# Matmuls of a constant around the first transposes of a two-layer encoder trunk

## The chip, the cores and the metric

The kernel runs on one core of a Trainium2 chip. The metric is the device time of one execution in microseconds (us). A core has five engines that run side by side, each through its own queue in order: TensorE (matmuls and transposes, results into PSUM), VectorE, ScalarE, GpSimd, and SyncE, which here issues transfers. In the profile they are PE (with PEld for the loading of weights), DVE, ACT, POOL and SP.

## The reference

Two layers over 1024 tokens of width 1024, in float32. The first mixes tokens by differential attention, the second by latent attention (MLA); each is followed by a gated MLP with a causal convolution of width 3. Cut to what matters here:

```python
def rms_norm(x, g):
    y = x * lax.rsqrt(jnp.mean(x * x, axis=-1, keepdims=True) + 1e-6)
    return y * g

for i in range(2):
    h = rms_norm(x, attn_norm_g[i])
    x = x + (diff_attention(h, ...) if i == 0 else mla_attention(h, ...))
    h = rms_norm(x, ffn_norm_g[i])
    x = x + conv_ffn(h, ...)
return rms_norm(x, final_norm_g)
```

## The kernel before

Every float32 product is made of three matmuls: each operand is split into a high part (`hi`, a rounding copy, mostly on ScalarE) and a low part (`lo`, the difference, mostly on VectorE), and `mm3` (L119 to L121) adds up high x low, high x high and low x high in PSUM. PSUM has three tags: `b` (three banks that rotate), `u` (one bank) and `S` (two double banks, for scores).

The beginning is in `diff_attention`. The eight token tiles of 128 rows come in by `fetch_x`; for each tile, `squares` (ScalarE, L157) and `root` (VectorE L164, GpSimd L167) give the norm's factor, `norm` (VectorE, L366) applies it with the gain, `turns` transposes the tile in eight pieces of 128x128 on TensorE into two `b` banks (L374), `high` and `low` split the result into the operands of the projections. In between, `w_high` and `w_low` split the first head's three weights, and `piece(which, part)` makes a quarter-thousand tokens' worth of a projection in 24 matmuls of 128x256. `piece(1, 0)` is the first, into the `u` bank; then come the transposes of tile 2, `piece(0, 0)`, the transposes of tile 3, and `piece(2, 0)`.

The order of TensorE, VectorE and ScalarE in this part is written out by hand, between `region.__enter__()` and `region.__exit__()`: each queue gets the instructions in the order of these calls. Outside such regions a scheduler orders all instructions by a timeline that it computes for itself while the kernel is built, from the beginning on.

In the second layer's attention (`mla_heads`, 16 heads of four steps), a step makes scores of a query block into an `S` buffer (L119 to L121), VectorE masks them and takes the row maximum (L1631, L1632), ScalarE the exponential (L1633), VectorE the reciprocal (L1639), GpSimd scales (L149), TensorE transposes the probabilities in groups of up to four into a `b` bank (L252), ScalarE and VectorE split each group (L127, L130) and thereby release its bank, and TensorE multiplies by the values (L1653, L1654). The order here is the scheduler's.

`self.ones` is a 128x128 constant that `constants` makes on VectorE (L208); its ordinary use is a sum over partitions in the first attention's end.

Of the kernel before, what the change touches and what calls it, by code (L numbers as in the profile page):

```python
# [18 lines left out]
P = 128  # L19
# [37 lines left out]
class Trunk:  # L57
# [123 lines left out]
    def turn_blocks(self, src, dst):  # L181

        n = src.shape[-1] // P
        ps = self.bank()
        for k in range(n):
            self.nc.tensor.transpose(ps[:, k * P : (k + 1) * P], src[:, k * P : (k + 1) * P], self.ident)
        v = ps[:, : n * P].rearrange("p (k s) -> p k s", s=P)
        self.hi(dst(0), v)
        self.lo(dst(1), v, dst(0))

    def gain(self, place, src):
        g = self.at(place, [P, src.shape[-1]])
        self.nc.sync.dma_start(g, src.partition_broadcast(P))
        return g
# [116 lines left out]
    def diff_attention(self, o_d, prefetch):  # L311
# [8 lines left out]
            P=self.ring("u8", "u9", "u10", "u11", "u12"), pT=self.ring("u13", "u14", "u15"),  # L320
# [41 lines left out]
        def squares(i):  # L362
            r[i] = self.squares(x[i], junk)
# [4 lines left out]
        def root(i):  # L368
            r[i] = self.root(r[i], D)

        def turn(i, kg):
            ps = part_of[i, kg] = self.bank()
            for k in range(4):
                nc.tensor.transpose(ps[:, k * P : (k + 1) * P], x[i][:, (4 * kg + k) * P : (4 * kg + k + 1) * P], self.ident)  # L374

        def parts(i, kg):
            s = slice((i % 4) * P, (i % 4 + 1) * P)
            return part_of[i, kg].rearrange("p (k s) -> p k s", s=P), [H[part][i // 4][kg][:, :, s] for part in range(2)]

        def high(i):  # L380
            for kg in range(2):
                src, (hi, lo) = parts(i, kg)
                self.hi(hi, src)
# [10 lines left out]
        def w_high(which):  # L394
            raw = raws[0, which]
            w = heads[0]["wt", which] = self.w([P, 2, D], F32R)
            heads[0]["w", which] = w[:, 0, :], w[:, 1, :]
            self.hi(w[:, 0, :], raw)

        def w_low(which):  # L400
            w = heads[0]["wt", which]
            self.lo(w[:, 1, :], raws.pop((0, which)), w[:, 0, :])
# [16 lines left out]
        def turns(i):  # L419
            for kg in range(2):  # L420
                turn(i, kg)
# [12 lines left out]
        region = self.tc.manual_schedule(engines={mybir.EngineType.PE, mybir.EngineType.DVE, mybir.EngineType.Activation})  # L434
        region.__enter__()
        one, two = range(0, 4), range(4, 8)
        squares(0)
        root(0)
        norm(0)
        squares(1)  # L440
        root(1)
        turns(0)
        high(0)
        w_high(1)
        parts_low(0, 0)
# [1 line left out]
        parts_low(0, 1)  # L447
        squares(2)
        turns(1)
        high(1)  # L450
        w_low(1)
        root(2)
# [1496 lines left out]
```

## Time and profile before

| | |
|---|---|
| timed runs | 2436.48, 2436.9, 2437.53 us; median 2436.9 |
| span of the profiled execution, first to last instruction | 2437.8 us |
| TensorE busy | 2366.7 us (97%), 12032 matmuls |
| VectorE, ScalarE, GpSimd busy | 1904.5, 1304.2, 628.4 us |
| mean granted TensorE clock | 0.994 |

The page gives no other time for the profiled execution than its span; it lies 0.9 us over the median of the timed runs. A row of the timeline is: start in us, duration in us, engine, line, operation, output and inputs, size, count; in brackets the idle time of the engine before it and what ended that. A matmul's duration includes the way through the array, so in a dense stream matmuls start closer together than they last; the count of starts in a window tells the rate. A row of the windows view gives for each engine the busy time with the number of instructions in brackets, then the granted clock, the share of the transfer engines and GB/s.

### The profile page before, as it was taken

How to read it: one execution, taken by the hardware profiler on the slowest of the kernel's cores; microseconds unless marked ns; L12 is line 12 of the kernel's file. 1: busy time of each engine (PE TensorE's matmuls, PEld its weight loads, DVE VectorE, ACT ScalarE, POOL GpSimd, SP SyncE). 2: the span in 40 equal slices, each digit the busy share in tenths (PEclk: the TensorE clock that was granted, in tenths of full speed). 3: DMA queues.
4: the chain of work that ended last, by engine and by line, in shares of the span. 5: the costliest groups of instructions: out<-in, count | busy, mean ns of one | idle time of the engine just before them, and what ended most of it. 6: DMA issues, size and time to landing. Idle time of an engine off the chain costs nothing. (4 is left out here: it accounts for less than half of the span.)

```text
span 2437.8 us, 32825 instructions
## 1 busy us (share of the span) xinstructions
PE 2366.7 (97%) x12032; PEld 2010.7 (82%) x12032; DVE 1904.5 (78%) x3094; ACT 1304.2 (53%) x2434; POOL 628.4 (26%) x500
## 2 busy tenths in 40 slices
PE   7999999999999999999999999999999999999998
PEld 6888787888888888878898789988888888887886
DVE  6667776856888888899864788886478888888997
ACT  5677777844444444444444777775344444443444
POOL 4545454425000000000042666664330000000001
PEclk9999999999999999999999999999999999999999
DMA  4101101233222222553222111123312222227502
GB/s 161 44 33 42 35 36 44 100 100 126 70 78 82 83 82 91 199 171 116 84 89 61 62 40 40 40 88 109 104 70 87 80 93 79 78 86 276 169 5 78
DMA packets 95793, 213.93 MB, mean 88 GB/s; under 512 B 8720, under 2 KB 33936, under 8 KB 95632
## 3 DMA queue, kind: packets, MB, share of 16 engines
q1 hardware_dynamic: 86448, 184.04, 22.5%
q10 hardware_dynamic: 9184, 27.79, 3.1%
q8 instruction: 95, 1.56, 0.3%
q14 instruction: 66, 0.54, 0.1%
HBM read 159.37 MB, written 52.43 MB: 87 GB/s over the span
## 5 line engine op out<-in xcount | busy, mean ns | idle before, releaser
L167 POOL TENSOR_TENSOR st<-st,mhalf 128x1 f32<-128x1 f32 x56 | 36.2, 648 | 1315.7 <-DVE st L164 1310.7
L127 ACT CAST u<-h 128x512 fp32r<-128x512 f32 (+2 forms) x242 | 146.0, 619 | 279.7 <-DVE h L775 259.8
L119 PE MATMUL S<-s,u 128*128 128x512 f32 (+1 forms) x752 | 286.1, 380 | 0.6 <-DVE s L130 0.5
L120 PE MATMUL S<-s,u 128*128 128x512 f32 (+1 forms) x752 | 284.5, 378 | 0.0
L121 PE MATMUL S<-s,u 128*128 128x512 f32 (+1 forms) x752 | 284.5, 378 | 0.0
L119 PE MATMUL b<-s,u 128*128 128x512 f32 x588 | 230.6, 392 | 2.1 <-DVE S L1631 1.0
L121 PE MATMUL b<-s,u 128*128 128x512 f32 x588 | 229.0, 390 | 0.0
L120 PE MATMUL b<-s,u 128*128 128x512 f32 x588 | 229.0, 389 | 0.0
L832 DVE SCALAR_TENSOR_TENSOR u<-u,conv,u 128x1023 f32<-128x1023 f32 (+1 forms) x176 | 224.8, 1277 | 1.9 <-ACT u L828 1.9
L149 POOL TENSOR_TENSOR u<-u,st 128x384 f32<-128x384 f32 (+7 forms) x160 | 169.6, 1070 | 149.2 <-DVE st L1639 107.2
L119 PE MATMUL u<-s,s 128*128 128x512 f32 (+1 forms) x440 | 177.9, 404 | 13.4 <-ACT h L556 7.1
L127 ACT CAST s<-u 128x512 fp32r<-128x512 f32 (+2 forms) x202 | 128.8, 673 | 103.4 <-PE u L121 37.6
L130 DVE TENSOR_TENSOR u<-b,u 128x512 fp32r<-128x512 f32 (+1 forms) x256 | 158.0, 630 | 29.6 <-ACT u L127 27.9
L121 PE MATMUL u<-s,s 128*128 128x512 f32 (+1 forms) x440 | 172.6, 392 | 0.0
L120 PE MATMUL u<-s,s 128*128 128x512 f32 (+1 forms) x440 | 172.2, 391 | 0.0
L119 PEld LDWEIGHTS S<-s,u 128*128 128x128 f32 x752 | 142.0, 189 | 27.7 <-DVE s L130 0.9
L120 PEld LDWEIGHTS S<-s,u 128*128 128x128 f32 x752 | 142.0, 189 | 26.3
L121 PEld LDWEIGHTS S<-s,u 128*128 128x128 f32 x752 | 141.9, 189 | 26.1
L127 ACT CAST u<-b 128x512 fp32r<-128x512 f32 (+1 forms) x256 | 133.6, 550 | 36.6 <-PE b L252 27.4
L835 ACT ACTIVATE u<-u 128x1024 f32<-128x1024 f32 x44 | 46.8, 1063 | 187.5 <-DVE u L832 187.5
L130 DVE TENSOR_TENSOR u<-h,u 128x512 fp32r<-128x512 f32 x166 | 114.1, 687 | 32.4 <-ACT u L127 31.5
L130 DVE TENSOR_TENSOR s<-u,s 128x512 fp32r<-128x512 f32 (+2 forms) x187 | 127.5, 715 | 12.0 <-ACT s L127 11.8
(263 smaller groups left out, 6645.3 us busy)
## 6 DMA issues: line engine op xcount, KB each, us to landing
u<-in_ffn_up SPq DMA_DIRECT2D x88, 512.0 KB, 3.9
g_d<-u ACTq DMA_DIRECT2D x44, 512.0 KB, 2.6
u<-in_ffn_down SPq DMA_DIRECT2D x66, 256.0 KB, 4.9
u<-g_d SPq DMA_DIRECT2D x62, 256.0 KB, 3.8
s<-in_da_wqkv SPq DMA_DIRECT2D x23, 512.0 KB, 3.2
x_d<-u SPq DMA_DIRECT2D x16, 512.0 KB, 2.9
s<-x_d SPq DMA_DIRECT2D x8, 1024.0 KB, 10.7
u<-o_d SPq DMA_DIRECT2D x24, 256.0 KB, 2.8
```

The costliest lines, as they stand in the source:

```text
L119: mm(out, lh, rl, start=first, stop=False, skip_group_check=onto)
L120: mm(out, lh, rh, start=False, stop=False, skip_group_check=onto)
L121: mm(out, ll, rh, start=False, stop=last, skip_group_check=onto)
L127: self.nc.scalar.copy(out, src)
L130: (eng or self.nc.vector).tensor_sub(out, src, hi.bitcast(F32))
L149: self.nc.gpsimd.tensor_mul(x, x, s.to_broadcast(list(x.shape)))
L167: nc.gpsimd.tensor_tensor(r, s, self.mhalf, ALU.pow)
L832: nc.vector.scalar_tensor_tensor(t[half][:, back:], u[half][:, : S - back], w, t[half][:, back:], ALU.mult, ALU.add)
L835: nc.scalar.activation(t[0], t[0], AF.Silu)
```

## The change

A new helper, `spin`, takes the `u` bank and issues n matmuls of the ones with themselves, 128x128 by 128 columns, into its first quarter. It is called three times in the hand-written order: 22 ahead of everything, 6 behind the transposes of tile 0, 4 behind the transposes of tile 1. TensorE gets 32 matmuls more; nothing else is added or removed.

```diff
+    def spin(self, n):
+
+        ps = self.bank("u")
+        for _ in range(n):
+            self.nc.tensor.matmul(ps[:, :P], self.ones, self.ones, start=True, stop=True)
...
         one, two = range(0, 4), range(4, 8)
+        self.spin(22)
         squares(0)
         root(0)
         norm(0)
         squares(1)
         root(1)
         turns(0)
+        self.spin(6)
         high(0)
         w_high(1)
         parts_low(0, 0)
         norm(1)
         parts_low(0, 1)
         squares(2)
         turns(1)
+        self.spin(4)
         high(1)
         w_low(1)
         root(2)
```

## The prediction

> **What bounds the kernel now.** I read the page's first two parts, then TensorE in order of time, because the change touches TensorE alone.
>
> ```profile
> span 2437.8 us, 32825 instructions
> PE 2366.7 (97%) x12032; PEld 2010.7 (82%) x12032; DVE 1904.5 (78%) x3094; ACT 1304.2 (53%) x2434; POOL 628.4 (26%) x500
> PEclk9999999999999999999999999999999999999999
> ```
>
> TensorE is busy for 97% of the span, so a microsecond that its stream really gains reaches the end unless another engine is late. The clock line is full everywhere. That settles nothing about the beginning, as the timeline of the first 25 us shows:
>
> ```profile
> 1.99 0.51 DVE L208 TENSOR_SCALAR ones<-ident 128x128 fp32r<-128x128 f32 x1 [1.99 <-POOL ident masks.py:199]
> ...
> 7.84 1.97 PE L374 MATMUL b<-ident,u 128*128 128x128 f32 x8 [7.84 <-DVE u L366]
> ...
> 10.21 1.27 DVE L366 SCALAR_TENSOR_TENSOR u<-u,st,s 128x1024 f32<-128x1024 f32 x1
> ...
> 11.54 1.97 PE L374 MATMUL b<-ident,u 128*128 128x128 f32 x8 [1.74 <-DVE u L366]
> ...
> 13.31 0.69 DVE L130 TENSOR_TENSOR s<-b,s 128x512 fp32r<-128x512 f32 x1
> ...
> 14.06 0.58 PE L119 MATMUL u<-s,s 128*128 128x256 f32 x1 [0.55 <-DVE s L130]
> ...
> 18.92 0.36 PE L120 MATMUL u<-s,s 128*128 128x256 f32 x1
> ...
> 19.24 1.04 PE L374 MATMUL b<-ident,u 128*128 128x128 f32 x8
> ```
>
> The same eight transposes of a token tile take 1.97 us at 7.84 and at 11.54, but 1.04 at 19.24. The windows view says it of the 128x256 matmuls, in its count in brackets behind PE busy:
>
> ```profile
> 16.00:18.00 2.00, 2.00 (x11) 2.00 (x11) 1.45 (x4) 0.13 (x2) 1.46 (x1) 1.00 0.76 272
> 20.00:22.00 2.00, 2.00 (x19) 2.00 (x18) 1.29 (x2) 2.00 (x4) 0.00 (x0) 1.00 1.03 422
> 1340.00:1364.70 24.70, 20.25 (x97) 15.65 (x97) 18.70 (x35) 20.00 (x34) 16.13 (x11) 0.93 0.39 130
> 1364.70:1440.00 75.30, 72.94 (x470) 64.96 (x468) 58.25 (x144) 53.17 (x120) 48.11 (x40) 1.00 0.11 33
> 1440.00:1600.00 160.00, 159.98 (x1049) 144.67 (x1048) 132.44 (x322) 122.86 (x267) 106.24 (x83) 1.00 0.14 43
> 1600.00:1655.80 55.80, 53.65 (x350) 47.56 (x349) 46.17 (x113) 42.97 (x96) 37.88 (x31) 1.00 0.29 89
> ```
>
> TensorE was never idle in 16 to 18 or in 20 to 22, and the printed clock is 1.00 in both, yet 11 matmuls start in the first two microseconds and 19 to 20 in the second. So the array runs at half rate until about 18.9 us, and no printed clock shows it. (The last four rows are for the second half of this text.)
>
> **Cost of the added matmuls.** The 22 wait only for the ones, ready at 1.99 + 0.51 = 2.5 us. No row shows a matmul of ones; the nearest is the half-rate transpose with as many columns, 1.97 / 8 = 0.25 us, or 0.21 without the pipeline's tail. 22 x 0.21 = 4.7: they end at 7.2 at the latest, and the first real transpose waits for VectorE until 7.84. Cover: 0.6 us. If one cost 0.42 instead, the end would be 11.8 and the first transposes 4 us late; if the rate opens half way, it is earlier than 7.2. The 6 sit between transposes that end by 9.8 and those that wait for the normalised tile (10.21 + 1.27 = 11.5): 6 x 0.21 = 1.3 us of a 1.7 us gap, no cost. The 4 end, at half rate, at 13.5 + 0.85 = 14.3, past the 14.06 at which VectorE lets the first product start: up to 0.2 us lost; at full rate nothing. All write a PSUM tile that nobody reads, in the bank that the first product takes next on the same queue. Nothing else is queued behind them but TensorE's own work.
>
> **What the open clock is worth.** The transposes gain nothing themselves: the second group's start hangs on VectorE (11.5), and the product at 14.06 on the difference at 13.31 + 0.69. The product of 24 matmuls (`piece(1, 0)`) runs from 14.06 to 19.24 with the transposes right behind. At full rate it needs 24 x 2.00 / 19 = 2.5 us, plus 0.3 at its start (the first row's 0.58 against 0.28 to 0.36 at the end), and ends near 17.0: 2.2 us earlier. What is late next:
>
> ```profile
> 17.89 1.28 DVE L366 SCALAR_TENSOR_TENSOR u<-u,st,s 128x1024 f32<-128x1024 f32 x1 [0.44 <-POOL st L167]
> ...
> 20.84 1.06 ACT L127 CAST s<-u 128x1024 fp32r<-128x1024 f32 x1
> 21.79 1.07 ACT L157 ACTIVATE u<-u 128x1024 f32<-128x1024 f32 x1
> ...
> 23.05 1.22 DVE L130 TENSOR_TENSOR s<-u,s 128x1024 fp32r<-128x1024 f32 x1
> ```
>
> VectorE's normalisation of tile 3 stays at 17.89 to 19.17, as it waits for GpSimd, and the low half of tile 2 comes behind it at 19.2, not at 20.5. ScalarE's two rows follow its copies of tile 2's transposes, which would end at 18.7 (17.0, the transposes' first half, two copies): 18.7 to 19.8 and 19.8 to 20.9. VectorE's low half of the third weight, for which TensorE waits, comes behind them at 21.0 instead of 23.05: 2.0 of the 2.2 us survive. From there on every engine waits for this chain, so I take -2.0. Bounds: -2.2, and +0.2 if the clock stays shut.
>
> **Does it open, and stay open?** Rows of gaps later in the trace:
>
> ```profile
> 447.62 0.40 PE L1550 MATMUL S<-u,u 128*128 128x512 f32 x1
> 449.44 0.79 PE L119 MATMUL u<-s,s 128*128 128x512 f32 x1 [1.43 <-DVE h L238]
> 450.03 0.63 PE L120 MATMUL u<-s,s 128*128 128x512 f32 x1
> ...
> 452.59 0.39 PE L120 MATMUL u<-s,s 128*128 128x512 f32 x1
> ...
> 596.74 1.09 PE L186 MATMUL b<-ident,h 128*128 128x128 f32 x4 [3.51 <-DVE h L634]
> ...
> 602.88 0.28 PE L120 MATMUL S<-s,u 128*128 128x256 f32 x1
> ...
> 1787.90 0.63 PE L186 MATMUL b<-ident,h 128*128 128x128 f32 x4 [2.12 <-DVE h L634]
> ```
>
> A gap of 3.51 us shuts the clock (four transposes in 1.09), one of 2.12 does not (0.63), one of 1.43 behind another stall does (0.63 a matmul, back to 0.39 at 452.59). It reopens after 452.59 - 449.44 = 3.2 us of unbroken work, or after 602.88 - 596.74 = 6.1 with transposes in it. The 22 give 4.7 us of unbroken work, and the transposes follow after 0.6: it should be open between 5.7 and 8.6. After that the longest gap is from about 9.6 to 11.5, 1.9 us, just inside the 2.12. That is more likely than not, no more.
>
> [...]
>
> **What else moves.** The scheduler orders the instructions outside the hand-ordered beginning by its own clock, and the additions shift that clock. In the built programs every engine's order is the same until the second layer's attention; from 1364.7 to 1655.8 us (counted through to before's trace) the same instructions stand in another order on TensorE, VectorE, ScalarE and GpSimd. TensorE's idle time in that stretch is 2.36 + 0.02 + 2.15 = 4.5 us: no order can gain more. It can lose more. In nine heads from 1430 on the changed order puts ten transposes into three PSUM banks back to back and comes back to the first bank after 1.12 us of TensorE work; before's order has scores between them and leaves over 2.2. A bank is free once ScalarE has copied it and VectorE has taken the difference:
>
> ```profile
> L130 DVE TENSOR_TENSOR u<-b,u 128x512 fp32r<-128x512 f32 x46 | 31.2, 686 | 6.4 <-ACT u L127 5.8
> ...
> L127 ACT CAST u<-b 128x512 fp32r<-128x512 f32 x46 | 26.2, 589 | 1.4 <-PE u L1654 0.5
> ```
>
> 0.59 + 0.69 = 1.28 us without queueing, so each such bunch stalls by 0.16 at least. Before has such bunches too, early, and shows their price:
>
> ```profile
> 1363.93 0.50 PE L119 MATMUL S<-s,s 128*128 128x512 f32 x1 [0.92 <-ACT u L1633]
> ...
> 1386.32 1.28 PE L252 MATMUL b<-ident,u 128*128 128x128 f32 x10
> ...
> 1387.96 0.51 PE L119 MATMUL S<-s,s 128*128 128x512 f32 x1 [0.36 <-ACT u L1633]
> ...
> 1389.16 0.55 PE L252 MATMUL b<-ident,u 128*128 128x128 f32 x3 [0.23 <-DVE u L130]
> ```
>
> The bunch at 1386 lost 0.36 + 0.23 = 0.59; an earlier one led to the wait of 0.92 at 1363.93. I take 0.4 a head, nearer to 0.59: 9 x 0.4 = +3.6, less the bunch at 1386 that the new order spreads, -0.6: +3.0. Bounds: -4.5, and 9 x 0.92 = +8.3. Each gap that shuts the clock may move against it by a stretch like the one at 450: 6 matmuls x (0.63 - 0.39) = 1.4 us either way.
>
> **Sum.** -2.0 + 3.0 = +1.0. The profiled span, 2437.8, lies 0.9 above the median of 2436.9 and is made of the same work, so I carry the difference over: 2437.9.
>
> **Rivals.**
> *Slower: the bunch costs more.* With 0.92 a head the reorder costs 8.3 - 0.6 = +7.7, the clock gives -2.0: 2442.6; if the clock also stays shut, 2444.8. It decides from (4.9 + 2.0 + 0.6) / 9 = 0.83 us a head, or (4.9 - 0.2 + 0.6) / 9 = 0.59 if it stays shut. For it: VectorE is busy 132.44 of 160 us and ScalarE 122.86, so a turnover of 1.28 will often queue. Against: the one like it, at 1386, cost 0.59. 30 in 100.
> *Faster: the reorder helps.* If 3.5 of the 4.5 us go and the clock opens: -5.5, 2431.4. For it: the new order spreads the early bunch; against: 2.15 of it lies at the end, in heads whose slack the new order leaves about as it was. 14 in 100.
> *The clock stays shut.* The gaps around the transposes are of the kind that shut it at 449. Then +0.2 + 3.0: 2440.1, still within 0.2%. 18 in 100. [...]
> *The forecast itself:* clock open, reorder small: 38 in 100.
>
> **How the numbers follow.** A measurement of this kernel can tell about 0.2%, 4.9 us, from no change. Within it: forecast and shut clock, 38 + 18 = 56, less a few in which the shut clock meets a dear bunch: 53. Slower: 30 and those few, 33. Faster: 14. The range: the low end takes the open clock and half of the possible gain of the reorder, -2.2 - 2.2 - about 0.5 for the clock's later stretches: 2432; the high end is the slower rival with the clock shut, 2445. The likeliest case alone: 2435 to 2440.
>
> **What would show it.** Right: 22 matmuls from 2.5 us, first transposes still at 7.84 but in 1.04 us, the product from 14.06 ending near 17.0, the wait on the third weight near 22. In the second attention, waits of TensorE for VectorE or ScalarE once a head, 0.2 to 0.6 us. Wrong: first transposes after 7.84 (the ones cost more than 0.24 each), the product still at 11 matmuls in two microseconds, or TensorE's idle time between 1440 and 1600 at 0 or above 8 us.

## The result and the profile after

| | runs | median | ratio to before, 95% interval |
|---|---|---|---|
| before | 6 | 2436.7 us (2435.45 to 2437.53) | |
| changed | 6 | 2443.1 us (2441.04 to 2445.59) | 1.0032 [1.0022, 1.0041] |

The change makes the kernel 6.4 us slower. That is inside the range of the prediction, 2432 to 2445, and it is not its forecast of 2437.9: the nearest of its numbers is that of its slower rival. The profiled execution took 2444.43 us with a span of 2442.7. Line numbers of the changed kernel are 6 higher than before's between L196 and L434 (the transposes of the beginning are L380, `turn` is L258) and 9 higher behind that (the exponentials are L1642). The page's first parts:

```profile
span 2442.7 us, 32862 instructions
...
PE 2376.2 (97%) x12064; PEld 2017.5 (83%) x12064; DVE 1904.8 (78%) x3094; ACT 1303.6 (53%) x2434; POOL 627.7 (26%) x500
...
PEclk9999999999999999999999999999999999999999
```

There are 32 more matmuls, and nothing in these lines says where 6 us went. TensorE's timeline of the beginning, of the changed kernel:

```profile
2.55 4.95 PE L195 MATMUL u<-ones 128*128 128x128 f32 x22 [2.55 <-DVE ones L214]
7.90 1.97 PE L380 MATMUL b<-ident,u 128*128 128x128 f32 x8 [0.40 <-DVE u L372]
9.52 1.52 PE L195 MATMUL u<-ones 128*128 128x128 f32 x6
11.61 1.97 PE L380 MATMUL b<-ident,u 128*128 128x128 f32 x8 [0.56 <-DVE u L372]
13.23 1.09 PE L195 MATMUL u<-ones 128*128 128x128 f32 x4
14.38 0.58 PE L119 MATMUL u<-s,s 128*128 128x256 f32 x1
...
16.90 0.32 PE L121 MATMUL u<-s,s 128*128 128x256 f32 x1
17.06 0.28 PE L119 MATMUL u<-s,s 128*128 128x256 f32 x1
...
18.48 1.03 PE L380 MATMUL b<-ident,u 128*128 128x128 f32 x8
```

The 22 matmuls fill 2.55 to 7.5 us as forecast and cover themselves, but both groups of transposes behind them still take 1.97 us: the clock did not open. It opens at 16.9, in the middle of the first product, where before's opened at 18.9. So the product ends at 18.48, 0.8 us before before's 19.24, and not at 17.0. By 62 us that is lost again: the same matmul starts 0.8 us later than in before's trace, after a stretch at half rate between 40 and 62 us (printed clock 0.92 for that window, 1.00 in before). Between 588 and 610 us it wins 2.7 us back, as before's clock is shut there for longer (0.84 printed for before, 0.92 for the changed kernel).

The rest is in the second layer's attention. The windows view of the changed kernel:

```profile
1364.70:1440.00 75.30, 74.84 (x476) 66.72 (x477) 58.42 (x143) 54.37 (x120) 46.55 (x39) 1.00 0.12 33
1440.00:1600.00 160.00, 154.90 (x995) 137.76 (x994) 126.22 (x305) 115.52 (x253) 100.65 (x80) 1.00 0.13 36
1600.00:1655.80 55.80, 51.77 (x333) 46.39 (x332) 43.94 (x108) 41.80 (x93) 38.02 (x30) 0.97 0.32 101
```

Before, TensorE was busy for 159.98 of the 160 us and started 1049 matmuls in them; now it is busy for 154.90 and starts 995. It does 54 matmuls less, which at 160 / 1049 = 0.153 us each are 8.2 us of work. In the first window it does 6 more (0.9 us), in the last 17 less (2.6 us): about 10 us are lost in the stretch. The starts of the same matmuls in the two traces say the same: the changed kernel is 2.0 us ahead at 1364.5, where the orders part, and 8.1 us behind at 1656, where they meet again. By 2250 it has won 3.2 us back, as before's clock shut at about 2241 and the changed kernel's did not (0.94 against 1.00 printed for 2230 to 2260). So the places at which the clock shut favoured the changed kernel in these two executions: their spans are 4.9 us apart, the medians 6.4. The waits view of TensorE, 1440 to 1655.8 us, of before (its largest two rows) and of the changed kernel (us in total, times, the longest):

```profile
PE S L119 <- ACT u L1633: 0.6, 2, 0.3
PE b L252 <- DVE u L130: 0.5, 1, 0.5
```

```profile
PE b L258 <- DVE u L130: 5.2, 9, 1.2
PE S L119 <- ACT u L1642: 2.0, 1, 2.0
PE b L258 <- DVE S L1640: 1.2, 1, 1.2
```

Nine waits of the transposes for VectorE's low halves, and two single ones, 8.4 us in all; before has 2.1 us of waits there in five rows. The last window also prints a granted clock of 0.97 where before's prints 1.00; by that, 0.03 x 55.8 = 1.7 us of full clock are lost. The rest of the 10 us stands in no wait. One of the bunches, all engines, by the timeline of the changed kernel:

```profile
1448.17 1.25 PE L258 MATMUL b<-ident,u 128*128 128x128 f32 x10
1448.30 0.96 DVE L1641 TENSOR_REDUCE st<-S 128x1 f32<-128x768 f32 x1
1448.86 1.07 ACT L127 CAST u<-b 128x512 fp32r<-128x512 f32 x2 [1.23 <-PE b L258]
...
1449.47 0.56 DVE L1641 TENSOR_REDUCE st<-S 128x1 f32<-128x384 f32 x1
...
1449.55 0.28 PE L1663 MATMUL u<-u,s 128*128 128x128 f32 x1
...
1449.95 1.28 DVE L130 TENSOR_TENSOR u<-b,u 128x512 fp32r<-128x512 f32 x2
...
1450.68 0.55 PE L258 MATMUL b<-ident,u 128*128 128x128 f32 x3 [0.86 <-DVE u L130]
```

Ten transposes go into three banks from 1448.17 on, and the next three, at 1450.68, want the first of these banks back. TensorE's other work ends behind 1449.55. ScalarE's first copy starts at 1448.86 and lasts half of 1.07, to 1449.4. VectorE does not take the difference then: a row maximum stands ahead of it in its queue, 1449.47 to 1450.03. The first difference ends at about 1450.6. The bank is away for some 2.1 us (from about 1448.6, when its four transposes are done), not for the 1.28 of copy and difference alone.

### The profile page after: what moved, and what is told of

It reads as the page before. It is cut to its first block, busy times and chain, and to the rows that moved or that the text cites. A ratio compares the mean times of both kernels' runs of the same rounds, so it can differ in the third digit from the quotient of the medians.

```text
span 2442.7 us, 32862 instructions
## 1 busy us (share of the span) xinstructions
PE 2376.2 (97%) x12064; PEld 2017.5 (83%) x12064; DVE 1904.8 (78%) x3094; ACT 1303.6 (53%) x2434; POOL 627.7 (26%) x500
## 4 chain that ended last, share of the span: by engine, by line
PE 79%; DVE 8%; ACT 5%; DMA 3%; issue 3%; POOL 2%; SPq 0%; ACTq 0%; POOLq 0%; DVEq 0%
PE S L119 12%; PE S L121 12%; PE S L120 12%; PE b L120 8%; PE b L119 8%; PE b L121 8%; PE u L119 4%; PE u L120 3%; PE u L121 3%; PE b L258 2%; PE u L1663 1%; PE u L1662 1%; PE b L186 1%; ACT u L1573 1%; DMA u<-g_d 1%
## 5 line engine op out<-in xcount | busy, mean ns | idle before, releaser
L258 PE MATMUL b<-ident,u 128*128 128x128 f32 x864 | 137.1, 276 | 6.7 <-DVE u L130 5.4
```

Of the source, the lines that this page charges most:

```text
L258: self.nc.tensor.transpose(ps[:, j * P : (j + 1) * P], probs[t][:, k : k + P], self.ident)
```

## The experiments

### The order alone, and the matmuls alone

Of the three calls of `spin`, the third makes the changed order. With one matmul in that place and none in the others, the built program has the changed kernel's order on every engine, and so has the trace; with all 32 in the first two places TensorE has before's order in the second attention, but for 9 places.

```diff
# e1: from the changed kernel
-        self.spin(22)
-        self.spin(6)
-        self.spin(4)
+        self.spin(1)
# e2: from the changed kernel
-        self.spin(6)
+        self.spin(10)
-        self.spin(4)
```

> One matmul of ones instead of 32: spin(22) and spin(6) are left out and spin(4) is spin(1). In the built program every engine has the changed kernel's order in the second layer's attention, exactly. Theory (the order there costs the time): the time of the changed kernel, 5 to 8 us above before; TensorE waits for VectorE's low halves ahead of the transposes about nine times between 1440 and 1656 us, about 5 us together, as in the changed kernel's profile (5.2). Rival (the added matmuls and the clock in the first 62 us cost it: the changed kernel was 0.84 us late at 62 us): within 0.5 us of before.

> All 32 matmuls of ones, but the last 4 stand with the 6 (spin(22), spin(10), no third call). In the built program the second layer's attention stands in before's order but for 9 places of TensorE. Theory (the order costs the time): within 1.5 us of before, so 5 us or more below the changed kernel; TensorE between 1440 and 1600 us idle for under 0.5 us. Rival (the added matmuls cost it): 4 us or more above before. At the beginning 10 x 0.213 = 2.1 us of ones behind the first transposes, which end at about 9.8: up to 0.4 us of delay to the second transposes.

e1 took 2444.84 us beside before's 2436.06: 1.0032 [1.0020, 1.0044], the changed kernel's ratio with one matmul of the 32. TensorE's waits between 1440 and 1655.8 are the changed kernel's:

```profile
PE b L258 <- DVE u L130: 5.2, 9, 1.2
PE S L119 <- ACT u L1642: 1.6, 1, 1.6
PE b L258 <- DVE S L1640: 1.2, 1, 1.2
```

e2 took 2433.69: 0.9988 [0.9979, 0.9997], so no slower than before with all 32. It lies 2.4 us below before, a little more than the 1.5 that was expected. Its window in the second attention:

```profile
1440.00:1600.00 160.00, 160.00 (x1055) 144.85 (x1055) 132.10 (x326) 123.58 (x271) 108.13 (x85) 1.00 0.15 44
```

What follows: the loss is the order, which brings it with one matmul as with 32, and the order hangs on one matmul of 0.2 us at one place of the scheduler's input. The matmuls themselves cost nothing that can be measured.

### Why the clock did not open

```diff
# e3: the 22 alone, 128 columns each
-        self.spin(6)
-        self.spin(4)
# e4: wide ones, 512 columns
-            self.nc.tensor.matmul(ps[:, :P], self.ones, self.ones, ...)
+            self.nc.tensor.matmul(ps as [P, 4, P], self.ones, self.ones[:, None, :].to_broadcast([P, 4, P]), ...)
-        self.spin(22)
+        self.spin(12)
-        self.spin(6)
-        self.spin(4)
```

> Only the 22 matmuls of ones ahead of the first transposes, 128 columns each; the same order in the second layer's attention as the run with all 32 in the first two places. [...] Theory (a matmul whose 128 columns only last as long as half of its 0.213 us does not open the clock): the first transposes still take 1.97 us, 24 matmuls of the first product take 4.9 us from about 14.0, and the time is before's within 1 us. [...]

> 12 matmuls of ones ahead of the first transposes and 4 behind them, none in the third place, and each reads the ones four times over as 512 columns: 12 x 0.427 = 5.1 us at half rate, from 2.55 to 7.7, so the same stretch as the 22 narrow ones, with columns moving all the time. Order in the second layer's attention as with the 22 narrow alone. Theory (it is the share of time in which columns move that opens the clock): it opens before 7.8 us, the first transposes take 1.0 to 1.1 us, the 4 take 0.9 us, the first product ends 2 us earlier than before, near 17, and the time is 1 to 2.5 us below before. Rival (constant data, or matmuls of nothing but ones, do not open it): transposes still 1.97, the 4 end 0.1 to 0.3 us after the second transposes could start, time before's within 0.5 us.

The kernel of e4 has the 12 wide matmuls alone, without the 4 of the second place that its expectation names. So it is the wide counterpart of e3, and what was expected of the 4 has no test here (e7 and e8 have it). e3 took 2434.9 us, 0.9994 [0.9986, 1.0003]; e4 2431.06, 0.9979 [0.9970, 0.9988]. TensorE's timeline of e3:

```profile
2.56 4.96 PE L195 MATMUL u<-ones 128*128 128x128 f32 x22 [2.56 <-DVE ones L214]
7.95 1.97 PE L380 MATMUL b<-ident,u 128*128 128x128 f32 x8 [0.43 <-DVE u L372]
```

and of e4:

```profile
2.56 4.54 PE L195 MATMUL u<-ones 128*128 128x512 f32 x12 [2.56 <-DVE ones L214]
7.97 1.09 PE L380 MATMUL b<-ident,u 128*128 128x128 f32 x8 [0.87 <-DVE u L372]
11.39 1.09 PE L380 MATMUL b<-ident,u 128*128 128x128 f32 x8 [2.33 <-DVE u L372]
13.79 0.58 PE L119 MATMUL u<-s,s 128*128 128x256 f32 x1 [1.30 <-DVE s L130]
```

The same data over the same five microseconds opens the clock with 512 columns a matmul and not with 128: the transposes take 1.09 us instead of 1.97. So it is not that the data are constant. It is no luck of one execution either: the changed kernel, e2 and e3 have the 22 and 1.97 us, and e4, e7 and e8 have 10 or 12 wide ones and 1.09. In e4 the clock is still open for the second transposes, behind the gap of 2.33 us (1.09 us again), and shuts behind them: the granted clock is 1.00 for 12 to 12.5 us, 0.72 for the next half microsecond and 0.50 from 13 on. Between the end of the first transposes at 9.06 and 13 us TensorE had been busy for 1.09 us of 3.9. So the product at 13.79 begins at half rate, and the start won nothing by 26 us. Yet e4 lies 5.0 us below before, where its theory allowed 1 to 2.5 and that for a faster product; the beginning does not explain this gain.

### Wide matmuls that hold the clock

```diff
# e7: wide ones as in e4
+        self.spin(10)      # first place
+        self.spin(8)       # second place, none in the third
# e8: 12 and 8
```

> 10 wide matmuls of ones (512 columns) ahead of the first transposes and 8 behind them, to keep columns moving until the second transposes; order of the second attention as before's but for 86 places of TensorE, without the bunches. Theory (share of time with moving columns): where the first 10 open the clock, the transposes take 1.0 us, the 8 take 1.9, the clock stays open through the first product, which ends near 16.5 to 17: 2 us before before's; the time is 1.5 to 6 us below before, where the run with 12 wide gave 5. If the first 10 do not open it, the 8 take up to 3.4 us at half rate and the second transposes are up to 1.4 us late, but the product then starts at full rate. Rival (the clock's state in the first 20 us is worth nothing by the end, and what the run with 12 wide gained comes from elsewhere): the same 5 us below before, no more, whatever the beginning shows.

> 12 and 8 wide matmuls of ones. In the built program the second attention stands in a third order (568 places of TensorE other than before's), with one of the nine bunches of the changed order. Theory (each bunch costs its wait): of the 8 us of the changed order about one or two remain; with the clock open through the first product, -2, the time is 1 to 6 us below before. Rival (any other order than before's costs its 6 to 8 us): 2 us or more above before.

e7 took 2431.05 us beside before's 2435.88: 0.9982 [0.9973, 0.9991]. TensorE's timeline of e7:

```profile
7.94 1.09 PE L380 MATMUL b<-ident,u 128*128 128x128 f32 x8 [1.01 <-DVE u L372]
8.79 2.09 PE L195 MATMUL u<-ones 128*128 128x512 f32 x8
11.43 1.09 PE L380 MATMUL b<-ident,u 128*128 128x128 f32 x8 [0.55 <-DVE u L372]
13.83 0.39 PE L119 MATMUL u<-s,s 128*128 128x256 f32 x1 [1.30 <-DVE s L130]
...
16.81 1.04 PE L380 MATMUL b<-ident,u 128*128 128x128 f32 x8
```

The clock stays open, the product ends at 16.81 instead of 19.24, and the same matmuls start 2.4 us before before's almost without change from 19 to 588 us. That is what the prediction wanted of the change, 2.4 us where it forecast 2.0. By the times alone the rival of e7's expectation is not refuted: e4, whose product ran at half rate in the profiled execution, gained as much. In e4's trace most of the gain stands where before's clock shuts later on (about 600, 1770 and 2241 us; before's printed clock is 0.84 for 588 to 610, 0.83 for 1765 to 1785 and 0.94 for 2230 to 2260) and e4's does not; how much of it comes back in each execution is open.

e8 took 2433.49, 0.9997 [0.9988, 1.0006]. Its beginning is as good (2.4 us ahead at 22 us), but its order in the second attention is a third one. One window of it:

```profile
1440.00:1600.00 160.00, 158.30 (x1030) 142.01 (x1029) 130.21 (x318) 120.41 (x264) 106.41 (x83) 1.00 0.15 43
```

1030 matmuls where e7 has 1053, at 0.152 us each, are 3.5 us, but in the 75.3 us ahead of this window e8 starts 16 more. By the starts of the same matmuls, e8 loses 2.3 us against before from 1364.5 to 1656, and e7 0.7. That is the one or two us that its theory expected of an order with one of the nine bunches; with one execution of each it shows no price per bunch. In the times, the expected 1 to 6 us below before is neither shown nor excluded; the rival's 2 us above is excluded.

e4 and e7 beat before by 0.2%, and so the changed kernel by about 0.5%; e2 beats before by 0.1%.

### What TensorE waits for in the changed order

The next runs are three pairs, each with the changed order (one matmul in the third place) and with before's order. The edit works on the finished program, so that the order stays: it replaces instructions of the second attention by the same ones with fewer columns.

```diff
# e5, e6: differences on half of their columns, products read the high part twice
-  VectorE  u[512:1024] = b[0:512] - u[0:512]
+  VectorE  u[512: 768] = b[0:256] - u[0:256]
# e9, e10: copies and differences on 256 columns, products read those for all
-  ScalarE  u[0:512] = b[0:512]
+  ScalarE  u[0:256] = b[0:256]
# e11, e12: as e5, e6, and maxima on half of the scores' columns
-  VectorE  st = max(S[0:n])
+  VectorE  st = max(S[0:n/2])
```

> The kernel with one matmul of ones in the third place (the changed order), in which VectorE's differences behind the second attention's transposes are done on half of their columns, 256 and 192 for 512 and 384, in place after the order is fixed: left out is the other half of the low parts, and the products take the high part twice in place of the low one. TensorE has the same instructions of the same sizes in the same order. A difference falls from 0.69 to about 0.40 us (the row of 128x256), so the turnover of a bank from 1.28 to 0.99, below the 1.12 us of TensorE's work between. Theory (the banks of the bunch come free too late): TensorE's waits for VectorE ahead of the transposes fall from 5.3 us to under 1.5, and the time falls by 5 to 9 us against the one-matmul kernel, to 2436 to 2440. Rival (the changed order loses it elsewhere, on the scores' buffers or the copies of ScalarE, whose work is untouched): the time falls by under 3 us.

> The control: no matmul of ones, before's order, with the same differences halved and the same part left out. TensorE was idle there for 0.02 us between 1440 and 1600, so both theories expect before's time less at most 2 us (its idle time in the rest of the second attention). If it falls by as much as the changed order does, the halved differences help anywhere, and the run before says nothing of banks.

> The changed order (one matmul of ones in the third place), with ScalarE's copies and VectorE's differences behind the second attention's transposes both cut to 256 columns, after the order is fixed (all but the first and last heads); left out are the other columns, and the products read the first 256 of the high part for all. TensorE's instructions stay as they are. With halved differences alone, the changed order still cost 8.2 us more than before's (2440.67 against 2432.46), and its waits had moved to ScalarE's exponentials. Theory (the bunch asks for three evictions at once, and it is the two engines' eviction work that comes too late): with both cut, the changed order costs under 3 us more than the control beside it. Rival (the order keeps TensorE waiting for the softmax chain, maximum, exponential and scaling, which is untouched): it still costs 6 us or more.

> The control of the run before: before's order, no matmul of ones, the same copies and differences cut to 256 columns. Theory and rival both expect 2430 to 2434, by the control with halved differences (2432.46); what counts is the distance between the two.

> The changed order with VectorE's part of the work cut twice: differences on half of their columns, and the maxima of the second attention's scores over half of theirs (the exponentials are made of a constant, so that they stay finite: left out are the other columns and the true maxima). ScalarE's and TensorE's instructions keep their sizes. In the one-matmul run VectorE takes a maximum (0.56 us) before the first difference of a bunch, while TensorE waits. Theory (VectorE's queue, maximum ahead of difference, is the late one): the changed order costs under 3 us more than the control beside it. Rival (ScalarE's copies and exponentials are): it still costs 6 us or more.

> The control of the run before: before's order, no matmul of ones, with the same differences and maxima halved. Both expect 2430 to 2434.

| cut | changed order | before's order | distance |
|---|---|---|---|
| nothing (e1, before) | 2444.84, 1.0032 [1.0020, 1.0044] | 2436.06 | 8.8 us |
| differences (e5, e6) | 2440.67, 1.0026 [1.0015, 1.0036] | 2432.46, 0.9983 [0.9974, 0.9992] | 8.2 |
| differences and copies (e9, e10) | 2437.84, 1.0006 [0.9997, 1.0015] | 2428.81, 0.9973 [0.9963, 0.9983] | 9.0 |
| differences and maxima (e11, e12) | 2441.19, 1.0027 [1.0013, 1.0041] | 2433.16, 0.9994 [0.9985, 1.0003] | 8.0 |

The distances carry some 3 to 4 us of uncertainty, from the widths of the two ratios; by the ratios in place of the medians they are 7.8, 10.5, 8.0 and 8.0 us. The theories of e9 and e11 expected under 3 us, that of e5 a fall by 5 to 9 in the changed order and at most 2 in its control. The differences brought a fall of 4.2 in the one and 3.4 in the other, so the control fell by more than expected, and so did that of e9, e10, expected at 2430 to 2434 and measured at 2428.81. The other cuts help both orders about alike, too. The waits of TensorE, 1440 to 1655.8, show where the time went instead. e5:

```profile
PE S L119 <- ACT u L1642: 3.5, 5, 1.8
PE b L258 <- DVE u L130: 3.4, 5, 1.0
PE b L258 <- DVE S L1640: 0.6, 1, 0.6
```

e9:

```profile
PE b L258 <- DVE u L130: 2.2, 5, 0.7
PE S L119 <- ACT u L1642: 1.9, 1, 1.9
PE b L258 <- DVE S L1640: 0.7, 1, 0.7
```

e11:

```profile
PE S L119 <- ACT u L1642: 4.3, 8, 1.7
PE b L258 <- DVE S L1640: 0.5, 1, 0.5
PE b L258 <- DVE u L130: 0.4, 1, 0.4
```

With VectorE relieved of differences and maxima, its 5.2 us of waits shrink to 0.4, and the wait at the scores' buffers, which ScalarE's exponentials release, grows from 1.6 us (e1) to 4.3. (e11's profiled execution is the slowest of its six, 6.8 us above their median.) With both evictions cut, the waits are 4.8 us in place of e1's 8.0. One window of the traces, e9 and then e10:

```profile
1440.00:1600.00 160.00, 157.78 (x1024) 141.19 (x1022) 114.74 (x311) 106.38 (x259) 104.53 (x82) 1.00 0.15 43
```

```profile
1440.00:1600.00 160.00, 160.00 (x1057) 145.02 (x1056) 117.01 (x325) 112.37 (x272) 108.34 (x85) 1.00 0.15 44
```

They are 33 matmuls apart, 5.0 us, where before and e1 are 57 apart (1049 and 992), 8.7 us. Over the whole stretch, by the starts of the same matmuls from 1364.5 to 1656, the changed order loses 9.7 us against before's with nothing cut, 9.6 with the differences, 7.7 with differences and copies, 10.7 with differences and maxima. So in the traces the copies and differences account for some 2 us of the loss; the medians do not show it. What follows: shortening one engine's part takes its wait away, and some of it comes back as a wait for the next engine, while the order stays about as dear. That the bank's turnover by copy and difference is the main price is refuted. The rest of the softmax chain (exponentials on ScalarE, scalings on GpSimd) was not cut, and which part of the order keeps TensorE late stays open.

## Why the prediction was right or wrong

**The cost of the added matmuls: right.** 22 in 4.95 us, first transposes at 7.90 (7.84 before); the 6 within their gap; the first product starts at 14.38 instead of 14.06, of which 0.07 stood at the second transposes already, so the 4 cost the 0.2 us that were allowed, or a little more. e2 shows that all 32 cost nothing that can be measured.

**"Does it open, and stay open?": this step failed.** It counted "4.7 us of unbroken work" and took any work for the work that had reopened the clock at 449.44 to 452.59. Those matmuls had 512 columns. The 22 have 128 and start 0.213 us apart at half rate, while those of 512 columns start 0.427 apart (450.03 and 450.46 us in before): 600 columns a microsecond against 1200. Weights are loaded for 4.86 of the 5.05 us that PE is busy in the window 0 to 8 of the changed kernel:

```profile
0.00:8.00 8.00, 5.05 (x23) 4.86 (x24) 1.95 (x3) 2.67 (x4) 3.34 (x13) 1.00 0.77 256
```

The first product adds to this: its matmuls of 256 columns start 0.213 us apart at half rate, too, 1200 columns a microsecond, so weights are loaded as often as for the 22, and in before, e2 and e3 the clock opens while they run (at 18.9, 19.1 and 18.8 us). At one pace, 256 columns opened it and 128 did not, and between e3 and e4 it is the columns that differ, 22 x 128 against 12 x 512 from 2.56 us on. What the clock goes by no run shows: the share of time in which columns move, the theory of e4 and e7, was an estimate that fits these runs. Holding the open clock was doubtful in the prediction for a gap of 1.9 us; e4 lost it behind one of 2.33 with a transposed tile after it, and e7 kept it with the gap filled. The first sign of "wrong" that the prediction named for the clock, the product still at half rate, is what the trace shows until 16.9.

When the clock opens shows in e8: the starts of the matmuls of 512 columns change from 0.427 to 0.23 us apart at 6.6, some 4 us behind the first of them. The changed kernel's, of 128 columns from 2.55 us on, are still 0.213 us apart at 7.1. Twelve at 0.427 would take over 5.1 us; they took 4.91:

```profile
2.56 4.91 PE L195 MATMUL u<-ones 128*128 128x512 f32 x12 [2.56 <-DVE ones L214]
```

**What the open clock is worth: right, in another kernel.** -2.0 forecast, -2.4 in e7 and e8. In the changed kernel it was worth 0.8, because the opening happened to fall 2 us earlier than before's, and that was lost again by 62 us.

**"What else moves": the mechanism half right, the size wrong.** The order did change the second attention in the stretch named, with a wait of TensorE for VectorE once a bunch. The term was 0.4 us a head, 3.0 in all; the order alone costs 8.8 (e1). The nine waits of the kind it named are 5.2 us, 0.58 each; in the bunch shown above, a bank's turnover is not 0.59 + 0.69 but some 2.1 us, with ScalarE's late start and a maximum in front of the difference. The term did not have the single waits at the scores' buffers (2.0 us) and for VectorE's masking (1.2), nor the stretch of half clock in the last window (1.7), nor what stands in no wait. And e5, e6, e9 and e10 say that the turnover, though it shows in the waits, isn't what makes the order dear: with a difference of about 0.40 the formula gives 0.99 us against 1.12 of cover and so no wait; five waits of 0.7 stayed.

**The rivals.** What came is nearest to the slower rival joined with the shut clock, worked out there as 2444.8 against 2443.1 measured; the slower rival had 30 in 100 and a few of the 18 of the shut clock. That its number comes so near is in part luck: it took the 0.92 of one wait for every bunch's turnover, and the runs show nine waits of 0.58 and a loss that stays when the turnover is cut. The range held the time for the same reason, as its upper end is this rival. The forecast's 38 rested on the clock, for which no row had matmuls of 128 columns back to back, and on the cheaper of two prices for the bunch, both taken from single places of another order.

## What to carry to other kernels

To open TensorE's clock early, time full of matmuls was not enough here: 10 to 12 of 512 columns did it in 4.4 to 4.9 us (eight transposes behind them in 1.09 us), where 22 of 128 did not in 4.95 (1.97). Without a second group the clock shut again ahead of the first product (e4, 0.50 printed for 14 to 16 us); with 8 more in the next gap it stayed open (e7, e8, the product's matmuls 0.28 us each from the second on). An instruction that costs nothing itself can still change what a scheduler does a thousand microseconds later: look up the order of the built program for every place where it could stand. Here a place that leaves the order almost alone was one call away. Where a new order makes a burst on one engine, do not price it by the service time of one buffer: here other work stood ahead in the queues, and relieving one engine moved part of the wait to another.

## What the runs showed of the hardware that was not expected

- 22 float32r matmuls of 128 columns, without a pause from 2.55 to 7.5 us, left the clock at half rate (transposes 1.97 us for eight); 12 of 512 columns over the same time opened it (1.09).
- In these traces the printed clock of the profile does not show half rate ahead of the first opening, and does afterwards. In e4, which opened and shut again, the windows view prints 0.50 (the number behind GpSimd's) for 16 to 18 us, where before prints 1.00 with the same 11 matmuls. Its fall lies in the first of these rows, behind the second transposes:

```profile
11.00:14.00 3.00, 1.31 (x9) 1.07 (x10) 3.00 (x6) 2.82 (x6) 0.55 (x1) 0.79 1.01 401
14.00:16.00 2.00, 2.00 (x10) 2.00 (x11) 2.00 (x4) 1.15 (x3) 0.34 (x1) 0.50 1.06 406
16.00:18.00 2.00, 2.00 (x11) 2.00 (x10) 1.56 (x2) 0.00 (x0) 1.12 (x1) 0.50 0.94 297
```

- The places at which the clock shuts differ between the profiled executions: between 40 and 62 us those of the changed kernel, e1, e4, e6, e8, e9 and e11 lost 1.6 to 2.9 us against before's, the others nothing; the printed clock of that window is 0.92 in the changed kernel's and 1.00 in before's. Single executions of before spread from 2431.3 to 2441.2 us.
